# Turning the rows of x in the prologue: products with a diagonal of reciprocal roots in place of a scaling pass and transposes

## The chip, the cores and the metric

The kernel runs on one core of a Trainium2 chip. The metric is device microseconds (us) of one execution. Three runs of the kernel before gave 1731.33, 1733.20 and 1735.08 us, median 1733.2. In the rows, PE is TensorE's matmul, PEld its weight load, DVE is VectorE, ACT is ScalarE, POOL is GpSimd and SP is the queue of SyncE, from which nearly all loads are issued. L248 is line 248 of the kernel before.

## What is computed

One decoder block on x of 1024 rows by 1024 channels, all in float32. Only the beginning matters here:

```python
mod = silu(c) @ w_ada + b_ada                      # 6 x 1024 numbers
sh1, sc1, g1, sh2, sc2, g2 = split(mod, 6)
h = rms_norm(x, norm_mix_g) * (1.0 + sc1) + sh1    # x * rsqrt(mean(x*x) + eps) * g ...
proj = h @ w_in + b_in                             # 1024 x 1024 times 1024 x 8200
```

After that come a gated convolution of 31 taps, a chunkwise mLSTM, merge gates, an output projection and a gated FFN. They are not touched.

## The kernel before

Every big product runs as three float32r products: an operand is split into a rounded part and a rest (`hi` and `lo` of the weights, `hh` and `hl` of h), and hi by hh, hi by hl and lo by hh are summed in PSUM. For such a product the contraction must lie on partitions, so h is needed turned: channels on partitions, rows along the free dimension. Eight tiles `xT[k]` of 128 channels by 1024 rows hold the turned, normalised x; `hh[k]` and `hl[k]` are made from them.

The prologue (lines 183 to 367) makes all that. Its parts, in the order of the code:

- Loads on SP, in this order: x (`xt`, four pieces of two row tiles), small parameter rows, the first group of the modulation weights (`wad`, `load_ada(0)`, 2 MB in four loads), two raw weight tiles of the first two product blocks (`raws`, L139), then `load_ada(1)` to `load_ada(3)`.
- For each half q of the rows (four row tiles): ACT squares and sums each tile (L235), DVE and POOL make the reciprocal roots (L237, L104), each row tile is scaled in place (L242 on ACT for one tile, L244 on DVE for seven), then for each of eight channel tiles k four transposes on PE fill one PSUM bank (L248, `pn` for k = 0, 3, 6, two buffers of `pc` for the others), and a copy moves the bank to `xT[k]` (L251). Of the 16 copies ACT makes 13 and DVE 3 (`EVAC`).
- `split_rest` makes hi and lo of the two raw weight tiles (L148 on ACT, L149 on DVE).
- The modulation in four groups g of two channel tiles. `mod_sums(g)` is eight DVE steps over `wad[g]` (L275, L277) into `macc`; `mod_products(g)` sums it over partitions with four float32 products by a column of ones (L283, eight records on PE); `mod_cols(g)` is four small ACT steps that make the columns `sh1` and `G1` (L292, L293).
- For each group then `high(k)` on ACT (`hh`, L297), `full(k)` on ACT (L300, in place on `xT`) and a subtraction on DVE (`hl`, L336); for the last group DVE makes the full value itself (L340, L343). `first_products(g, 0)` is 16 products with `hh` and `first_products(g, 1)` eight with `hl` (L308), for the first two blocks at once, into two PSUM tiles `first[0]` and `first[1]`.

The order on each engine is written out by hand: three lists `on_v`, `on_s` and `on_t` hold groups of instructions for DVE, ACT and PE, and `in_turn` queues each group behind the one before it. On PE the order is `first_products(g, 0)`, `mod_products(g + 1)`, `first_products(g, 1)`. On DVE it is, for each g, `mod_sums(g + 1)` and then the two subtractions. What is in no list is placed by the planner of the language, by its own model of durations. Last, `param_columns` turns four tiles of later parameter rows through the single PSUM buffer `pa` (L125, L128).

After the prologue `glu_gate` reads `first[0]` on ACT (a sigmoid, L412), which frees the PSUM tile into which the third block of products (L158) runs. From there on PE works almost without a break to the end.

Of the kernel before, what the change touches and what calls it, by code (L numbers as in the profile page):

```python
# [17 lines left out]
KT = 8  # L18
# [17 lines left out]
SCALE = "vvvvvvva"  # L36
EVAC = ("aaaaaaaa", "avaavaav")
# [11 lines left out]
def hybrid_block(ctx: ExitStack, tc: tile.TileContext, x, c, w_ada, b_ada, norm_mix_g, w_in, b_in,  # L49
# [72 lines left out]
    def param_columns(rows):  # L122
        group, plan, t = rows
        p = ps_a()
        nc.tensor.transpose(p[:, 0:128], t, ident)  # L125
        n = sum(n for _, _, n in plan)
        col = const.tile([128, n], F32, name=f"col{group}")
        nc.vector.tensor_copy(col, p[:, 0:n])  # L128
        at = 0
        for key, ap, n in plan:  # L130
            cols[key] = col[:, at:at + n]
            at += n
# [52 lines left out]
    rows = pro.tile([128, 8, 128], F32, name="rows", tag="rows", bufs=2)  # L185
# [3 lines left out]
    xt = []  # L189
# [25 lines left out]
    def split_rest():  # L215
        for i in range(2):
            load_split(None, 0, KT, 0, *w_first[i], raw=raws[i])
# [11 lines left out]
    late_evac = {"v": [], "s": []}  # L229
    rstd = pro.tile([128, 3, 8], F32, name="rstd")  # L230
    xT = [big.tile([128, S], F32, name=f"xT{k}", tag="xb") if k < XB else pro.tile([128, S], F32, name=f"xT{k}") for k in range(KT)]
    for q in range(2):
        for t in range(4 * q, 4 * q + 4):
            junk = ps_mm()
            nc.scalar.activation(flat(junk), xt[t], AF.Square, accum_out=rstd[:, 0, t:t + 1])  # L235
        ms, rs, sc = (rstd[:, i, 4 * q:4 * q + 4] for i in range(3))
        nc.vector.tensor_scalar(ms, ms, 1.0 / D, EPS, op0=OP.mult, op1=OP.add)  # L237
        rsqrt(rs, ms)
        for t in range(4 * q, 4 * q + 4):
            r = rstd[:, 1, t:t + 1]  # L240
            if SCALE[t] == "a":
                nc.scalar.activation(xt[t], xt[t], AF.Copy, scale=r)  # L242
            else:
                (nc.gpsimd if SCALE[t] == "p" else nc.vector).tensor_scalar(xt[t], xt[t], r, None, op0=OP.mult)  # L244
        for k in range(KT):
            p = ps_n() if k % 3 == 0 else ps_c()
            for t in range(4):
                nc.tensor.transpose(p[:, t * 128:(t + 1) * 128], xt[q * 4 + t][:, k * 128:(k + 1) * 128], ident)  # L248
            h = xT[k][:, q * 512:(q + 1) * 512]
            e = "s" if EVAC[q][k] == "a" else "v"  # L250
            ins = nc.scalar.activation(h, p, AF.Copy) if e == "s" else nc.vector.tensor_copy(h, p)  # L251
            if q and k > 1:
                late_evac[e].append(ins)
# [48 lines left out]
    def first_products(g, kind):  # L302
        ks = (2 * g, 2 * g + 1)
        x = hl if kind else hh
        steps = [(i, k, n) for n in ((0,) if kind else (0, 1)) for k in ks for i in range(2)]
        if g == 3 and kind:
            steps.sort(key=lambda step: step[0])
        return [nc.tensor.matmul(flat(first[i])[:, a:b], w_first[i][n][:, k, :], x[k][:, a:b],  # L308
                                 start=(g == 0 and k == 0 and n == 0 and not kind), stop=(g == 3 and k == KT - 1 and kind == 1))
                for i, k, n in steps for a, b in HALVES]  # L310
# [5 lines left out]
    on_v.append(parts[1])  # L316
    on_v.append(late_evac["v"])
    on_s.append(late_evac["s"])
    split_rest()
    p, ins = mod_products(0, acc)  # L320
    for g in range(4):
# [8 lines left out]
        else:  # L330
            w_next[0] = wp.tile([128, KT, 128], F32R, name="whi", tag="whi"), wp.tile([128, KT, 128], F32R, name="wlo", tag="wlo")
            raw_next = load_raw(win, 0, KT, GLU_B + 128)
        if g < 3:
# [11 lines left out]
        if g == 2:  # L345
            rows = pro.tile([128, 8, 128], F32, name="rows", tag="rows", bufs=2)
# [11 lines left out]
        on_t.append(first_products(g, 0))  # L358
        if g < 3:
# [5 lines left out]
    for rows in later:  # L365
        param_columns(rows)
# [970 lines left out]
```

## Time and profile before

| | us |
|---|---|
| median of three runs | 1733.2 |
| profiled execution, its own time | 1735.88 |
| its span, first instruction to last | 1734.1 |
| PE busy in the span | 1692.9 (98%) |
| DVE busy | 1249.7 (72%) |
| ACT busy | 611.7 (35%) |
| start of the first L158 product | 61.59 |

The span of the profiled execution is 1.8 us shorter than its time, which is what lies around it. In a row of the timeline the columns are start and duration in us, engine, line, operation, what is written and read, how many were merged, and in brackets the idle time before with what ended it. The granted clock is a share of TensorE's full speed of 2.4 GHz. Ends of matmuls are modelled, so pace is read from starts.

### The profile page before, as it was taken

Reading aid. Unit: us, or ns where it says so; the run is one execution under the profiler, and the core shown is the slowest. Engines: PE = TensorE matmul, PEld = TensorE weight load, DVE = VectorE, ACT = ScalarE, POOL = GpSimd, SP = SyncE. Lnnn points to the kernel's source line nnn. Section 1 sums busy time; section 2 is a strip of 40 time slices with the busy share of each in tenths; the row PEclk is TensorE's granted clock in tenths of the full one; section 3 lists DMA queues with packets and bytes.
Section 4 is the critical chain, followed back from the end, with each engine's and each line's share of the span. In section 5 each row is a group of like instructions: output and inputs, shape, how many; then the busy total and the mean of one; then the engine's idle time right before and its main releaser. Section 6 shows DMA issues by size and latency. Waiting matters only on the chain. (4 is left out here: it accounts for less than half of the span.)

```text
span 1734.1 us, 20875 instructions
## 1 busy us (share of the span) xinstructions
PE 1692.9 (98%) x8360; PEld 1418.6 (82%) x8360; DVE 1249.7 (72%) x1681; ACT 611.7 (35%) x809; POOL 52.7 (3%) x113
## 2 busy tenths in 40 slices
PE   5999999999999999999999998999999999999998
PEld 4788889888988888888888778888888888778887
DVE  6989998997799669446798668766666665685243
ACT  7424335323433253223522386322222222232122
POOL 0000001000001000000000000000000000000000
PEclk9999999999999999999999999999999999999999
DMA  9221120221111112243694743322222222653121
GB/s 320 63 62 49 37 71 28 61 73 49 37 49 61 61 49 61 73 146 98 209 376 167 230 152 104 98 86 85 86 73 75 84 81 96 226 168 101 58 94 52
DMA packets 194711, 179.91 MB, mean 104 GB/s; under 512 B 7463, under 2 KB 166711, under 8 KB 194615
## 3 DMA queue, kind: packets, MB, share of 16 engines
q1 hardware_dynamic: 177367, 146.61, 27.4%
q10 hardware_dynamic: 17248, 31.99, 5.0%
q8 instruction: 65, 1.06, 0.3%
q14 instruction: 31, 0.25, 0.0%
HBM read 146.06 MB, written 32.51 MB: 103 GB/s over the span
## 5 line engine op out<-in xcount | busy, mean ns | idle before, releaser
L388 DVE SCALAR_TENSOR_TENSOR cacc<-a,col,cacc 128x1024 f32<-128x1024 f32 x240 | 306.8, 1286 | 3.9 <-ACT cacc L386 1.4
L158 PE MATMUL mm<-hh,wlo 128*128 128x512 f32 x864 | 271.2, 391 | 1.5 <-DVE wlo L149 1.5
L158 PE MATMUL mm<-hl,whi 128*128 128x512 f32 x864 | 272.5, 392 | 0.0
L158 PE MATMUL mm<-hh,whi 128*128 128x512 f32 x864 | 271.6, 392 | 0.0
L158 PEld LDWEIGHTS mm<-hh,wlo 128*128 128x128 f32 x864 | 160.3, 188 | 33.6 <-DVE wlo L149 2.7
L158 PEld LDWEIGHTS mm<-hl,whi 128*128 128x128 f32 x864 | 161.0, 188 | 32.1 <-issue 0.5
L158 PEld LDWEIGHTS mm<-hh,whi 128*128 128x128 f32 x864 | 160.5, 188 | 31.6
L148 ACT ACTIVATE whi<-wraw 128x1024 fp32r<-128x1024 f32 x61 | 64.7, 1061 | 226.5 <-PE mm L158 171.3
L149 DVE TENSOR_TENSOR wlo<-wraw,whi 128x1024 fp32r<-128x1024 f32 x61 | 74.5, 1222 | 28.7 <-ACT whi L148 25.2
L1114 PE MATMUL mm<-Bh,gh 128*128 128x512 f32 (+1 forms) x192 | 71.5, 375 | 2.9 <-ACT gh L1051 1.5
L1115 PE MATMUL mm<-Bl,gh 128*128 128x512 f32 (+1 forms) x192 | 71.5, 373 | 0.6 <-DVE Bl L1033 0.6
L604 PE MATMUL mm<-wlo,hh 128*128 128x256 f32 x256 | 72.0, 282 | 0.0
L1116 PE MATMUL mm<-Bh,gl 128*128 128x512 f32 (+1 forms) x192 | 71.2, 371 | 0.0
L1303 DVE TENSOR_TENSOR x<-x,mm 128x1024 f32<-128x1024 f32 x24 | 29.3, 1219 | 52.0 <-PE mm L1301 49.6
L1179 ACT ACTIVATE whi<-wraw 128x512 fp32r<-128x512 f32 (+2 forms) x32 | 25.3, 792 | 114.8 <-PE mm L1301 75.8
L535 DVE SCALAR_TENSOR_TENSOR cacc<-qkraw,col,cacc 128x1024 f32<-128x1024 f32 x48 | 61.5, 1282 | 4.9 <-ACT cacc L533 4.5
L603 PE MATMUL mm<-whi,hh 128*128 128x256 f32 x192 | 54.6, 284 | 0.0
L605 PE MATMUL mm<-whi,hl 128*128 128x256 f32 x192 | 54.2, 283 | 0.0
L1299 PE MATMUL mm<-fa,whi 128*128 128x512 f32 x128 | 50.6, 396 | 1.6 <-DVE cu L1142 0.9
L1300 PE MATMUL mm<-fa,wlo 128*128 128x512 f32 x128 | 50.5, 395 | 1.2 <-DVE wlo L1180 1.2
L1301 PE MATMUL mm<-fa,whi 128*128 128x512 f32 x128 | 50.6, 395 | 0.0
L1052 DVE TENSOR_TENSOR ul<-uraw,uh 128x1024 fp32r<-128x1024 f32 x20 | 24.5, 1225 | 35.4 <-ACT uh L1051 35.4
(444 smaller groups left out, 3893.1 us busy)
## 6 DMA issues: line engine op xcount, KB each, us to landing
wraw<-in_w_in_dram SPq DMA_DIRECT2D x64, 512.0 KB
awt<-in_w_ada_dram SPq DMA_DIRECT2D x32, 512.0 KB
graw<-in_w_ffn_up_dram SPq DMA_DIRECT2D x24, 512.0 KB
uraw<-in_w_ffn_up_dram SPq DMA_DIRECT2D x22, 512.0 KB
draw<-in_w_ffn_down_dram SPq DMA_DIRECT2D x22, 512.0 KB
act_d<-cg ACTq DMA_DIRECT2D x38, 256.0 KB
wad<-in_w_ada_dram SPq DMA_DIRECT2D x16, 512.0 KB
wraw<-in_w_out_dram SPq DMA_DIRECT2D x16, 512.0 KB
```

What stands on the lines that cost most here:

```text
L148: nc.scalar.activation(hi, raw, AF.Copy)
L149: (eng or nc.vector).tensor_sub(lo, raw, hi.bitcast(F32))
L158: nc.tensor.matmul(flat(acc)[:, a:b], lhs[:, k, :], rhs[k][:, a:b], start=(first and k == 0), stop=(last and k == kt - 1))
L388: nc.vector.scalar_tensor_tensor(acc, a[:, j:j + S], dw_col(j, ct), acc, op0=OP.mult, op1=OP.add)
L535: nc.vector.scalar_tensor_tensor(cv, raw[:, j:j + S], wcol(j), cv, op0=OP.mult, op1=OP.add)
L603: nc.tensor.matmul(o, hh[k][:, ts_], his[k], start=False, stop=False)
L604: nc.tensor.matmul(o[:, 0:256], hh[k][:, ts_], los[k], start=False, stop=False)
L605: nc.tensor.matmul(o, hl[k][:, ts_], his[k], start=False, stop=(k == KT - 1))
L1114: nc.tensor.matmul(o, a, rh, start=(k == 0), stop=False)
L1115: nc.tensor.matmul(o, a, rl, start=False, stop=False)
L1116: nc.tensor.matmul(o, b, rh, start=False, stop=(k == 3))
L1299: nc.tensor.matmul(o, hi[:, i, :], his[i][:, a:b], start=(i == 0), stop=False)
```

## The change

The scaling of the row tiles is gone. DVE instead makes, for each row tile, a 128x128 diagonal matrix of that tile's reciprocal roots (`diag`), and PE multiplies each block of x by it: a float32 product of a block with a diagonal is the block turned and scaled. All 16 copies out of PSUM are ACT's. In the written order DVE has all eight sums of group 0 first, then the lo parts of the first weights. PE has five of the second half's eight banks ahead of `mod_products(0)` and the other three between `first_products(0, 0)` and `mod_products(1)`. ACT has two of the second half's copies ahead of `mod_cols(0)`, three after `high(1)` and three ahead of `mod_cols(1)`. In the last group the products with `hh` and `hl` are reordered so that `first[0]` is complete eight products before the end. The tile `rows` has one buffer where it had two, and the last four turns of parameter rows go to four PSUM buffers. The diff, cut to its core:

```diff
-    rows = pro.tile([128, 8, 128], F32, name="rows", tag="rows", bufs=2)
+    rows = pro.tile([128, 8, 128], F32, name="rows", tag="rows")
...
     def split_rest():
+        out = []
         for i in range(2):
-            load_split(None, 0, KT, 0, *w_first[i], raw=raws[i])
+            hi, lo = w_first[i]
+            nc.scalar.activation(hi, raws[i], AF.Copy)
+            out.append(nc.vector.tensor_sub(lo, raws[i], hi.bitcast(F32)))
+        return out
...
+    diag = pro.tile([128, 8, 128], F32, name="diag")
...
         for t in range(4 * q, 4 * q + 4):
-            r = rstd[:, 1, t:t + 1]
-            if SCALE[t] == "a":
-                nc.scalar.activation(xt[t], xt[t], AF.Copy, scale=r)
-            else:
-                (nc.gpsimd if SCALE[t] == "p" else nc.vector).tensor_scalar(xt[t], xt[t], r, None, op0=OP.mult)
+            nc.vector.tensor_scalar(diag[:, t], ident, rstd[:, 1, t:t + 1], None, op0=OP.mult)
         for k in range(KT):
             p = ps_n() if k % 3 == 0 else ps_c()
-            for t in range(4):
-                nc.tensor.transpose(p[:, t * 128:(t + 1) * 128], xt[q * 4 + t][:, k * 128:(k + 1) * 128], ident)
-            h = xT[k][:, q * 512:(q + 1) * 512]
-            e = "s" if EVAC[q][k] == "a" else "v"
-            ins = nc.scalar.activation(h, p, AF.Copy) if e == "s" else nc.vector.tensor_copy(h, p)
-            if q and k > 1:
-                late_evac[e].append(ins)
+            turned = [nc.tensor.matmul(p[:, t * 128:(t + 1) * 128], xt[q * 4 + t][:, k * 128:(k + 1) * 128], diag[:, q * 4 + t],
+                                       start=True, stop=True) for t in range(4)]
+            copied = nc.scalar.activation(xT[k][:, q * 512:(q + 1) * 512], p, AF.Copy)
+            if q:
+                turns.append(turned)
+                copies.append([copied])
...
+        if g == 3:
+            if not kind:
+                return []
+            high = [(i, k, n, hh) for n in (0, 1) for k in ks for i in range(2) if n == 0 or i == 0]
+            steps = high + [s for s in steps if s[0] == 0] + [(1, k, 1, hh) for k in ks] + [s for s in steps if s[0] == 1]
...
-    on_v.append(parts[1])
-    on_v.append(late_evac["v"])
-    on_s.append(late_evac["s"])
-    split_rest()
+    on_v += parts
+    on_v.append(split_rest())
+    on_s += copies[:2]
+    on_t += turns[:5]
     p, ins = mod_products(0, acc)
+    on_t.append(ins)
...
+        if g == 0:
+            on_s += copies[2:5]
...
         on_t.append(first_products(g, 0))
+        if g == 0:
+            on_t += turns[5:]
+            on_s += copies[5:]
...
-    for rows in later:
-        param_columns(rows)
+    for rows, bank in zip(later, (ps_a, ps_n, ps_c, ps_c)):
+        param_columns(rows, bank)
```

## Rows read from the trace of the kernel before

**Rows 1.** The page: the span.
```profile
span 1734.1 us, 20875 instructions
```

**Rows 2.** Windows: start:end, length, busy us of each engine (x instructions), clock, DMA, GB/s.
```profile
16.50:26.90 10.40, 7.08 (x52) 5.46 (x52) 9.65 (x14) 9.46 (x16) 1.02 (x1) 1.00 1.13 328
26.90:30.90 4.00, 1.12 (x10) 0.99 (x9) 3.89 (x8) 2.10 (x6) 0.00 (x0) 0.90 1.09 348
30.90:37.00 6.10, 6.10 (x14) 4.76 (x15) 5.85 (x7) 3.33 (x3) 0.00 (x0) 0.50 1.09 349
37.00:61.60 24.60, 23.79 (x112) 18.00 (x110) 22.87 (x30) 18.30 (x26) 0.22 (x2) 1.00 0.42 115
61.60:1734.00 1672.40, 1651.30 (x8163) 1386.82 (x8162) 1202.71 (x1607) 567.05 (x740) 49.74 (x103) 1.00 0.31 98
```

**Rows 3.** Timeline of PE: sums over partitions, products of the first blocks, third block.
```profile
27.71 1.05 PE L283 MATMUL pa<-ones_col,macc 128*128 128x1 f32 x8 [0.77 <-DVE macc L277]
30.88 6.74 PE L308 MATMUL mm<-hh,wf 128*128 128x512 f32 x16 [2.12 <-ACT hh L297]
37.46 0.95 PE L283 MATMUL pa<-ones_col,macc 128*128 128x1 f32 x8
...
51.58 1.04 PE L283 MATMUL pa<-ones_col,macc 128*128 128x1 f32 x8
...
58.86 1.99 PE L308 MATMUL mm<-hl,wf 128*128 128x512 f32 x8
...
61.59 0.73 PE L158 MATMUL mm<-hh,whi 128*128 128x512 f32 x2
```

**Rows 4.** Timeline of DVE: the last seven sums of group 3.
```profile
46.04 5.47 DVE L277 SCALAR_TENSOR_TENSOR macc<-wad,sc_c,macc 128x512 f32<-128x512 f32 x7
```

**Rows 5.** Lines of DVE, 0 to 62 us: count, busy us, mean ns, idle before.
```profile
L277 DVE SCALAR_TENSOR_TENSOR macc<-wad,sc_c,macc 128x512 f32<-128x512 f32 x28 | 21.0, 751 | 0.9
L336 DVE TENSOR_TENSOR hl<-xT,hh 128x1024 fp32r<-128x1024 f32 x6 | 7.3, 1221 | 0.3
L244 DVE TENSOR_SCALAR xt<-xt,rstd 128x1024 f32<-128x1024 f32 x7 | 4.8, 748 | 1.6 <-POOL rstd L104 1.6
...
L251 DVE COPY xT<-pc 128x512 f32<-128x512 f32 x3 | 2.0, 688 | 0.0
...
L237 DVE TENSOR_SCALAR rstd<-rstd 128x4 f32<-128x4 f32 x2 | 0.3, 170 | 1.9 <-ACT mm L235 1.9
```

**Rows 6.** Timeline of PE: transposes early and later.
```profile
12.85 0.48 PE L248 MATMUL pn<-ident,xt 128*128 128x128 f32 x1 [3.84 <-DVE xt L244]
13.11 0.63 PE L248 MATMUL pc<-ident,xt 128*128 128x128 f32 x2
...
19.88 1.14 PE L248 MATMUL pc<-ident,xt 128*128 128x128 f32 x8
```

**Rows 7.** Timeline of PE near 792 us: float32 products of 512 columns.
```profile
792.40 1.02 PE L832 MATMUL pn<-t4b,ones_d 128*128 128x512 f32 x2
793.26 1.02 PE L832 MATMUL pc<-t4b,ones_d 128*128 128x512 f32 x2
```

**Rows 8.** Timeline of ACT: a weight split, columns and high parts, the sigmoid.
```profile
23.35 1.06 ACT L148 ACTIVATE wf<-wraw 128x1024 fp32r<-128x1024 f32 x1 [0.23 <-DMA wraw<-in_w_in_dram]
...
28.80 0.26 ACT L292 ACTIVATE sh<-pa,mod_b 128x1 f32<-128x1 f32 x1 [2.07 <-PE pa L283]
...
29.58 2.38 ACT L297 ACTIVATE hh<-xT,sh,G 128x1024 fp32r<-128x1024 f32 x2
...
55.70 1.06 ACT L341 ACTIVATE whi<-wraw 128x1024 fp32r<-128x1024 f32 x1
...
60.42 1.11 ACT L412 ACTIVATE t<-mm,col 128x1024 f32<-128x1024 f32 x1 [1.41 <-PE mm L308]
```

**Rows 9.** Lines of ACT, 0 to 62 us: copies out of PSUM.
```profile
L251 ACT ACTIVATE xT<-pc 128x512 f32<-128x512 f32 x7 | 3.9, 593 | 0.3 <-PE pc L248 0.3
```

**Rows 10.** Timeline of SP: the issue of the next raw weights.
```profile
45.34 1.01 SPq L139 DMA_DIRECT2D wraw<-in_w_in_dram  x2
```

More of the change, by code (lines that the diff above doesn't have):

```diff
@@ L35 @@
 AT = (43, 43, 46, 49, 20, 20, 49, 49, 17, 24, 66, 64)
-SCALE = "vvvvvvva"
-EVAC = ("aaaaaaaa", "avaavaav")
 KX = 6
@@ L120, in param_rows, with param_columns @@
         return group, plan, t
-    def param_columns(rows):
+    def param_columns(rows, bank=ps_a):
         group, plan, t = rows
-        p = ps_a()
+        p = bank()
         nc.tensor.transpose(p[:, 0:128], t, ident)
@@ L227, in dw_col @@
         return cols["dw0"][:, r:r + 1] if r < 128 else cols["dw1"][:, r - 128:r - 127]
-    late_evac = {"v": [], "s": []}
+    turns, copies = [], []
     rstd = pro.tile([128, 3, 8], F32, name="rstd")
+    diag = pro.tile([128, 8, 128], F32, name="diag")
     xT = [big.tile([128, S], F32, name=f"xT{k}", tag="xb") if k < XB else pro.tile([128, S], F32, name=f"xT{k}") for k in range(KT)]
@@ L235, in hybrid_block @@
             nc.scalar.activation(flat(junk), xt[t], AF.Square, accum_out=rstd[:, 0, t:t + 1])
-        ms, rs, sc = (rstd[:, i, 4 * q:4 * q + 4] for i in range(3))
+        ms, rs = (rstd[:, i, 4 * q:4 * q + 4] for i in range(2))
         nc.vector.tensor_scalar(ms, ms, 1.0 / D, EPS, op0=OP.mult, op1=OP.add)
@@ L304, in first_products @@
         x = hl if kind else hh
-        steps = [(i, k, n) for n in ((0,) if kind else (0, 1)) for k in ks for i in range(2)]
-        if g == 3 and kind:
-            steps.sort(key=lambda step: step[0])
+        steps = [(i, k, n, x) for n in ((0,) if kind else (0, 1)) for k in ks for i in range(2)]
+        if g == 3:
[3 more added lines that the diff above has]
+            steps = high + [s for s in steps if s[0] == 0] + [(1, k, 1, hh) for k in ks] + [s for s in steps if s[0] == 1]
         return [nc.tensor.matmul(flat(first[i])[:, a:b], w_first[i][n][:, k, :], x[k][:, a:b],
-                                 start=(g == 0 and k == 0 and n == 0 and not kind), stop=(g == 3 and k == KT - 1 and kind == 1))
-                for i, k, n in steps for a, b in HALVES]
+                                 start=(g == 0 and k == 0 and n == 0 and x is hh),
+                                 stop=(g == 3 and k == KT - 1 and x is hl))
+                for i, k, n, x in steps for a, b in HALVES]
     on_v, on_s, on_t = [], [], []
@@ L345, in hybrid_block @@
         if g == 2:
-            rows = pro.tile([128, 8, 128], F32, name="rows", tag="rows", bufs=2)
+            rows = pro.tile([128, 8, 128], F32, name="rows", tag="rows")
             later = [
```

## The prediction, made before the change was run

> **What bounds the kernel now.** I read the span first [rows 1], then the windows [rows 2]: after 61.6 us PE is busy 1651.3 of 1672.4 us, so nearly all that is left there is PE's own work, and what the prologue costs is the time at which the third block starts, 61.59 [rows 3]. A change in the prologue is worth what it moves that start. In 37.0 to 61.6 DVE is busy 22.9 of 24.6 us and PE 23.8 [rows 2]: two engines are nearly full, and the order of waits must say which is late.
>
> The timeline of PE gives the frame [rows 3]: sums over partitions (`mod_products`, below mp0 to mp3) start at 27.71, 37.46 and 51.58; mp1 to mp3 are 14.1 us for two groups, 7.06 each. The first waits for DVE's `macc`. The last starts 0.07 after DVE ends the last sum of group 3, 46.04 + 5.47 = 51.51 [rows 4]. So at both ends DVE is the late one. One group costs DVE eight sums (about 0.5 + 5.47 = 6.0) and two subtractions of 1.22, 8.4 us together [rows 4, 5], more than the 7.06 that PE and ACT take in turn; DVE is behind them at mp3 because it began late, at about 51.5 - 6.0 - 2 x 8.4 = 28.7. From mp3 to the third block it is 10.0 us: the last product of the prologue ends at 58.86 + 1.99 = 60.85, but the third block waits until the sigmoid (60.42 + 1.11 = 61.53) frees a PSUM tile [rows 3, 6].
>
> **What goes.** Seven scalings on DVE, 4.8 us, three copies, 2.0 us [rows 5], and one scaling on ACT. A diagonal of 128x128 on DVE costs between 0.17 (the 128x4 form) and 0.75 (the 128x1024 form it replaces) [rows 5]; in proportion to its columns I take 0.2, eight are 1.6. DVE loses about 5.2 us. ACT gains three copies of 0.59 [rows 7], 0.5 from start to start: 1.5 less the scaling. The first turn waits for one diagonal instead of one scaling and starts near 12.3 instead of 12.85 [rows 8].
>
> **What a turn costs on PE.** Two float32 products of 512 columns start 0.86 us apart, two records each [rows 9]; a quarter of the columns is 0.215 per product. Eight transposes take 1.14, about 0.12 each in their banks [rows 8]. A bank of four turns thus goes from 0.5 to 0.9 us with a little for the change of bank. This is at full clock. The first transposes come slower, two in 0.63 [rows 8], and the stretch from 30.9 to 37.0 is granted 0.50 (1.2 GHz) after PE was busy 1.12 us in the 4.0 before; from 16.5 it is granted 1.00 (2.4 GHz) [rows 2]. At the lower level a bank costs 1.7.
>
> A rule that speaks against the change: the Trainium skill (TensorE: Matmul & The Clock Gate, Terms) calls the transpose mode four times faster for FP32. By it a product would cost 4 x 0.12 = 0.5, a bank 1.9 and 13 banks 25 us, an estimate; the rows here give less than twice. What that would do is the mechanism of the slower rival below.
>
> **The sum, step by step.**
> - mp0 now stands behind thirteen banks. From 12.3 at the lower level to 16.5 are 2.4 banks; the other 10.6 at 0.9 take until 26.0. Bounds: 24.0 at full level throughout, 34.5 at the lower. The sums of group 0, first on DVE now, end near 24 and don't bind. I take 26.0 to 26.5, against 27.71.
> - From mp0 to the first product it was 30.88 - 27.71 = 3.2 us (records, four column steps, one `high`) [rows 3, 6]; nothing of that changes: 29.3.
> - The pause between mp0's end and that product stays 2.1 us [rows 3], now after dense work. Before, the sixteen products after it took 6.58 instead of 16 x 0.23 = 3.6 [rows 3]. I take half of the slow stretch, 5.3, so 34.6. Then come the three late banks, 2.7, and mp1 is at 37.2 against 37.46. Bounds: 35.5 at full level, 39.4 with the whole slow stretch of 6.1 us.
> - DVE meanwhile. The second raw weight tile lands at 23.35 [rows 6]; `wad(1)`, 2.1 MB at 348 GB/s [rows 2], 6.0 us later at 29.4, its first half at 26.4. The last four sums of group 1 then end at 29.4 + 3.2 = 32.6. The subtractions need `full(0)` on ACT: columns at 27.3, two `high` of 1.14, three copies of 0.5, `full(0)` of 1.14 give 33. Sums of group 2 run from 35.3 to 41.3, some 1.8 earlier than before (51.5 - 6.0 - 2.4 - 6.0 = 37.1). But `full(2)` comes mp1 + 5.2 = 42.4 (records 1.0, columns 0.8, three passes of 1.14): DVE waits 1.1, which gives most of it back. Sums of group 3 end at 42.4 + 2.4 + 6.0 = 50.8; PE by its own turn comes to mp3 at 37.2 + 14.1 = 51.3 or a little less. I take 51.0, 0.6 earlier.
> - The tail. `first[0]` is complete eight products, 1.8 us, before the end, which covers 1.11 of sigmoid and the latency seen. The wait of 61.59 - 60.85 = 0.7 goes; PE's own products are late next.
> Sum: 0.6 + 0.7 = 1.3 us. At full level throughout DVE doesn't wait for `full(2)`: mp3 at 49.6, 2.0 + 0.7 = 2.7. With the whole slow stretch mp3 is at 53.4 and the sum 1.1 us later than before.
>
> Costed at nothing, with their cover: the four late turns of parameter rows and their copies (PE's pauses; 0.3 us each if they come in line); the two memsets of the second `rows` tile, which now waits until the first is read near 15 us (0.17 each on DVE); the loads behind them on SP, among them the next raw weights, issued at 45.34 [rows 10] and read at 55.70 [rows 6], with some 5 us of room after they land. On ACT a weight split queued ahead of copies would hold them until the tile lands; the PSUM banks give it about one bank, 0.9.
>
> The sum is made on the profiled execution, 1735.88 us, which would be 1734.6; that execution lies 2.7 above the median of the three runs, so I carry the difference over: 1733.2 - 1.3 = 1731.9.
>
> **Rivals.** This kernel's measurement can tell about 0.2%, 3.5 us, from no change.
> - Full clock: the pause of 2.1 us doesn't lower the grant. For it: PE is denser before the pause than it was. Against: 26.9 to 30.9 [rows 2], where 1.12 us of work in 4.0 was followed by 0.50. 1733.2 - 2.7 = 1730.5.
> - Slower: turns decide. If PE runs the products at the lower level to the end, or a product costs four transposes, mp0 is at 34.5 and everything after it 8 us later; the sum is 6 to 9 us against it, 1740.7. The point from which it decides: gain is gone when mp0 is 1.3 later than taken, at 27.5, so when thirteen banks take over 15.2 us, 1.17 each. For it: the early pairs of transposes at 0.63. Against: transposes already raised the grant by 16.5, and products are denser.
> - Nothing: ACT, with more copies and the same splits, or the late parameter turns on PE, hand back 1.3 us. 1733.2.
> - More: DVE, 5.2 us lighter, goes into the long part with a lead. There PE has 21 us without work [rows 2]; if a quarter goes, 1731.9 - 5 = 1726.9. Against: PE follows its own order there, and that idle time is in small pieces behind many engines.
>
> **How the numbers follow.** Forecast 52%, full clock 20%, slower 7%, nothing 13%, more 8%. The predicted time is the forecast's, 1731.9. Its own bounds reach from 1730.5 to 1734.3; the three runs of before differ by up to 1.9 from their median, so the range is 1728.0 to 1735.5, which leaves out most of the slower and the larger case and some of the edges. Faster by over 3.5 us: all of the largest case, about half of the full clock's, a tenth of the forecast's, 0.23. Slower by over 3.5: the slower case and 2% from the edges, 0.09. Within: 0.68.
>
> **What would show it.** Right: turns of 0.2 us per product from about 17 us on, mp0 between 25.5 and 27, `full(0)` and then DVE's subtractions near 33, a DVE wait for `full(2)` of about 1 us, mp3 near 51, no wait of PE between `first[1]` and the third block, and that block at 60.3. Wrong: mp0 after 27.5 (the turns), sums of group 1 late (the loads), mp3 before 49.5 (something else bound it), or a start near 60.3 with a median that has moved by more than 3 us: then the long part has changed.

## The result, and the profile after

The changed kernel is slower, by 0.2 to 0.3%. Against runs of the kernel before its median was 1739.03 us to 1732.78 (eight runs each). The comparison puts the ratio at 1.0028 with a 95% interval of 1.0019 to 1.0037; the bare ratio of the two medians, 1.0036, lies near the upper end of it. Two later comparisons gave 1.0028 (1.0018 to 1.0038) and 1.0021 (1.0012 to 1.0030). The forecast was 1731.9 with a range of 1728.0 to 1735.5, so the time moved the other way and lies outside the range. In the rows section four groups stand under other numbers than the prediction gives them: its [rows 6] is the group printed as Rows 8, its 7 is Rows 9, its 8 is Rows 6 and its 9 is Rows 7; this section and the next ones use the printed numbers.

The profiled execution of the changed kernel took 1735.75 us. It is the fastest of its eight and as long as the profiled one of before (1735.88), so the two profiles compared whole show no loss; what they do show is where the time goes in the prologue. Lines of its page and its windows, in the columns of [rows 2] (line numbers are always those of the kernel that ran: L246 here is L248 of the kernel before):

```profile
span 1734.0 us, 21003 instructions
PE 1697.1 (98%) x8424; PEld 1425.0 (82%) x8424; DVE 1244.6 (72%) x1679; ACT 611.4 (35%) x811; POOL 52.5 (3%) x113
...
16.50:26.90 10.40, 10.40 (x87) 10.27 (x86) 8.61 (x21) 7.43 (x12) 1.02 (x1) 1.00 1.13 328
26.90:30.90 4.00, 1.88 (x15) 1.66 (x13) 3.42 (x6) 2.88 (x6) 0.00 (x0) 1.00 1.09 350
30.90:37.00 6.10, 6.10 (x26) 4.84 (x25) 5.86 (x8) 4.22 (x7) 0.00 (x0) 0.72 1.09 349
37.00:61.60 24.60, 23.04 (x116) 17.54 (x115) 22.00 (x29) 18.72 (x28) 0.00 (x0) 1.00 0.36 104
61.60:1734.00 1672.40, 1651.03 (x8170) 1386.28 (x8168) 1202.66 (x1607) 566.83 (x741) 49.82 (x105) 1.00 0.31 99
```

DVE has become lighter, as it should: 1244.6 us busy in the span where it had 1249.7, 5.1 for the 5.2 put down. PE now works through all of 16.5 to 26.9, and in 37.0 to 61.6 it is a little less busy than before (23.04 us for 23.79). What counts is PE's timeline, which answers to [rows 3] and [rows 6]:

```profile
12.31 0.80 PE L246 MATMUL pn<-diag,xt 128*128 128x128 f32 x2 [3.20 <-DVE diag L243]
...
16.74 1.06 PE L246 MATMUL pc<-diag,xt 128*128 128x128 f32 x4
...
18.74 1.95 PE L246 MATMUL pc<-diag,xt 128*128 128x128 f32 x16
20.53 1.06 PE L246 MATMUL pn<-diag,xt 128*128 128x128 f32 x8
...
27.03 0.95 PE L281 MATMUL pa<-ones_col,macc 128*128 128x1 f32 x8
30.09 5.74 PE L309 MATMUL mm<-hh,wf 128*128 128x512 f32 x16 [2.12 <-ACT hh L295]
...
38.34 0.95 PE L281 MATMUL pa<-ones_col,macc 128*128 128x1 f32 x8
...
43.33 0.31 PE L123 MATMUL pn<-ident,rows 128*128 128x128 f32 x1 [0.72 <-DMA rows<-in_conv_dw_w_dram]
...
46.26 0.27 PE L123 MATMUL pc<-ident,rows 128*128 128x128 f32 x1
47.03 0.30 PE L123 MATMUL pc<-ident,rows 128*128 128x128 f32 x1 [0.51 <-DMA rows<-in_qk_conv_w_dram]
47.17 0.95 PE L281 MATMUL pa<-ones_col,macc 128*128 128x1 f32 x8
...
54.24 0.95 PE L281 MATMUL pa<-ones_col,macc 128*128 128x1 f32 x8
...
61.30 1.98 PE L309 MATMUL mm<-hl,wf 128*128 128x512 f32 x8
64.03 0.73 PE L156 MATMUL mm<-hh,whi 128*128 128x512 f32 x2 [0.75 <-ACT t L420]
```

The third block starts at 64.03 instead of 61.59: 2.44 us later, where 1.3 earlier was forecast. Read the four sums over partitions (L281): mp0 is 0.68 earlier than before and mp1 0.88 later. Between mp1 and mp2 lie 8.83 us, where before every group took 7.06, and from mp2 to mp3 it is 7.07 again. So it is the stretch from 38.3 to 47.2 that is too long, and three instructions stand in it that were not there before: L123, turns of the late parameter rows. Two of them wait for their loads, 0.72 and 0.51 us. DVE's timeline shows copies of such turns, which wait for PE in their turn, and the sums of group 3 behind the second:

```profile
43.68 0.29 DVE L126 COPY col<-pn 128x128 f32<-128x128 f32 x1 [1.36 <-PE pn L123]
...
47.38 0.29 DVE L126 COPY col<-pc 128x128 f32<-128x128 f32 x1 [0.35 <-PE pc L123]
47.58 5.47 DVE L275 SCALAR_TENSOR_TENSOR macc<-wad,sc_c,macc 128x512 f32<-128x512 f32 x7
```

The queue of SP shows when these loads are issued, the first and the last of twelve, and under them the last one in the kernel before:

```profile
37.10 0.36 SPq L116 DMA_DIRECT2D rows<-in_conv_dw_w_dram  x1
...
44.55 0.55 SPq L116 DMA_DIRECT2D rows<-in_qk_conv_w_dram  x1
```

```profile
44.06 0.55 SPq L118 DMA_DIRECT2D rows<-in_qk_conv_w_dram  x1
```

The load that the turn at 43.33 waits for was issued at 37.1 or 38.5, while the `wad` loads still filled the DMA engines (share 1.09 in the row up to 37.0). The turn that reads the last load can't come before about 47, 2.5 us after its issue; mp2 was wanted at 45.4 (38.34 + 7.06). The Trainium skill (DMA: Bandwidth & Descriptors, section Anatomy of one DMA — SWDGE (gpsimd) path) gives a transfer a fixed cost of about 2.0 us, measured there for GpSimd's issue; these rows, on SP's, show 2.5 from the start of the issue (44.55) and 1.9 from its end (45.10) to the product that waits for it (47.03), which agrees with it roughly.

Last the tail. The sigmoid that answers to the one of [rows 8] still waits for PE:

```profile
62.86 1.11 ACT L420 ACTIVATE t<-mm,col 128x1024 f32<-128x1024 f32 x1 [1.28 <-PE mm L309]
```

It starts 0.42 before PE's last product ends (61.30 + 1.98 = 63.28), just as before (60.42 against 60.85), and the third block waits 0.75 for it.

### The profile page after: what moved, and what is told of

Its sections match the earlier page's. It is cut to its first block, busy times and chain, and to the rows that moved or that the text cites. A ratio compares the mean times of both kernels' runs of the same rounds, so it can differ in the third digit from the quotient of the medians.

```text
span 1734.0 us, 21003 instructions
## 1 busy us (share of the span) xinstructions
PE 1697.1 (98%) x8424; PEld 1425.0 (82%) x8424; DVE 1244.6 (72%) x1679; ACT 611.4 (35%) x811; POOL 52.5 (3%) x113
## 4 chain that ended last, share of the span: by engine, by line
PE 87%; DVE 5%; DMA 4%; issue 2%; SPq 2%; ACT 1%; POOL 0%; POOLq 0%; ACTq 0%; DVEq 0%
PE mm L156 39%; PE mm L1122 5%; PE mm L1123 4%; PE mm L1124 4%; PE mm L1308 2%; PE mm L1309 2%; PE mm L1307 2%; PE mm L611 1%; PE mm L613 1%; PE mm L612 1%; PE pc L1122 1%; PE pc L1124 1%; PE pc L1123 1%; SPq L199 1%; PE pa L1123 1%
## 5 line engine op out<-in xcount | busy, mean ns | idle before, releaser
L543 DVE SCALAR_TENSOR_TENSOR cacc<-qkraw,col,cacc 128x1024 f32<-128x1024 f32 x48 | 61.5, 1282 | 5.0 <-ACT cacc L541 4.5
```

## The experiments

All comparisons are with runs of the kernel before on the same chip; a1 and e1 to e3 ran on one chip, the other runs of the table on a second. The ratio is that of the comparison and can differ a little from that of the two medians. "Third block" is the start of the first product behind the prologue and "rest" is the span less that, both from the one profiled execution. Before has 61.59 and 1672.6. The diffs are cut to what matters, with `...` for what is left out.

| label | what it is | median us (runs) | before | ratio, 95% interval | third block | rest |
|---|---|---|---|---|---|---|
| a1_after_again | changed kernel | 1738.78 (9) | 1734.08 | 1.0028 (1.0018 to 1.0038) | 63.88 | 1673.9 |
| e1_one_bank | changed, late turns through one buffer | 1738.77 (10) | 1734.08 | 1.0023 (1.0014 to 1.0032) | 61.62 | 1674.3 |
| e2_late | changed, late turns queued late | 1735.37 (11) | 1734.08 | 1.0011 (1.0003 to 1.0020) | 62.36 | 1671.3 |
| e3_before_banks | before, four buffers for the late turns | 1736.30 (11) | 1734.08 | 1.0010 (1.0001 to 1.0019) | 65.95 | 1670.1 |
| e4_products_only | before, turns by products | 1737.19 (11) | 1734.32 | 1.0016 (1.0007 to 1.0025) | 64.14 | 1671.3 |
| e6_pause | changed, three repairs | 1736.05 (11) | 1734.32 | 1.0009 (1.0000 to 1.0018) | 61.22 | 1674.5 |
| e8_old_order | e1 with the order of before behind the prologue | 1734.86 (11) | 1734.32 | 1.0008 (0.9998 to 1.0017) | 62.14 | 1673.3 |
| e9_new_order | before with e1's order behind the prologue | 1735.46 (11) | 1734.32 | 1.0009 (1.0000 to 1.0018) | 61.61 | 1671.6 |
| e10_after_old_order | changed with the order of before behind the prologue | 1738.15 (11) | 1734.13 | 1.0020 (1.0011 to 1.0029) | 64.02 | 1672.0 |
| e11_before_new_order | before with the changed kernel's order behind the prologue | 1734.45 (11) | 1734.13 | 1.0001 (0.9992 to 1.0010) | 61.48 | 1670.2 |
| a2_after_third | changed kernel | 1738.10 (11) | 1734.13 | 1.0021 (1.0012 to 1.0030) | 63.73 | 1669.4 |
| a0_before_again | before | 1734.95 (11) | 1734.13 | 1.0004 (0.9995 to 1.0012) | 61.53 | 1672.6 |

### The late turns of parameter rows

The theory after the first profile: the four PSUM buffers let the planner place the late turns ahead of mp2, where they wait for loads. Its rivals were that the products with the diagonals themselves cost the time, and that it is lost behind the prologue. The changed kernel ran again beside three edits:

> The changed kernel once more, unchanged. Its first profile has the third block at 64.03 us, 2.44 later than before, and a granted clock of 0.998; most of its other executions were granted 0.994 to 0.996 and took 3 us more. Theory 'prologue': the loss of about 6 us in the median is the 2.4 us of the prologue and the grant, which falls more often than before; a second profile then shows the third block within 0.5 us of 64.0 and further stretches at 0.50, and the spans go with the grant, some 1.7 us per stretch of 3.4 us. Theory 'long part': the loss lies after the third block at equal grant; then the stretch from the third block to the end is over 1671 us even where the grant is 1.00 in it (1670.0 in the first profile).

e1_one_bank takes the late turns back to the one buffer `pa`, which the sums over partitions use as well:

```diff
-    for rows, bank in zip(later, (ps_a, ps_n, ps_c, ps_c)):
-        param_columns(rows, bank)
+    for rows in later:
+        param_columns(rows)
```

> The changed kernel, with the four late turns of parameter rows through the one buffer pa again, as before; all else of the change stays. Theory 'late rows': with free PSUM buffers the planner queues three of these turns on PE ahead of mp2 (and their copies on DVE among the subtractions and the sums), where they wait for their loads; PE lost about 1.8 us there (8.83 us from mp1 to mp2 instead of 7.06). Then mp2 comes 7.1 after mp1, the third block at 61.5 to 62.2, and the median 1.5 to 3 us below the changed kernel's. Theory 'products': the dear turns on PE lose the time; then the third block stays within 0.5 us of 64.0.

e2_late keeps the four buffers and writes down where the turns stand, on PE behind the products of group 2 and on DVE behind the subtractions:

```diff
         on_t.append(first_products(g, 1))
+        if g == 2:
+            late_cols = [param_columns(rows, bank) for rows, bank in zip(later, (ps_a, ps_n, ps_c, ps_c))]
+            on_t.append([turn for turn, _ in late_cols])
...
+            on_v.append([late_cols[0][1]])
...
+            on_v.append([copy for _, copy in late_cols[1:]])
...
-    for rows, bank in zip(later, (ps_a, ps_n, ps_c, ps_c)):
-        param_columns(rows, bank)
```

> The changed kernel with four buffers, but the four late turns queued by hand on PE behind the products of group 2 with hl, and their copies on DVE behind the last subtractions. Theory 'late rows': as with one buffer, mp2 7.1 after mp1 and the third block at 61.5 to 62.3. Theory 'products': no change within 0.5 us. If the number of buffers matters by itself (a bank not free in time), this one is late and the one with a single buffer is not.

e3_before_banks gives the kernel before the four buffers, and nothing else of the change:

```diff
-    def param_columns(rows):
+    def param_columns(rows, bank=ps_a):
...
-        p = ps_a()
+        p = bank()
...
-    for rows in later:
-        param_columns(rows)
+    for rows, bank in zip(later, (ps_a, ps_n, ps_c, ps_c)):
+        param_columns(rows, bank)
```

> The kernel before, with only the four buffers for the late turns of parameter rows. Theory 'late rows': the planner does the same here, some turns stand ahead of mp2 or mp3 and wait for their loads; the third block comes 1 to 3 us after 61.59 and the median rises by as much. If the four buffers only help, as the prediction held, PE's 0.4 us wait for pa is gone and the third block comes at 61.2 to 61.6.

PE's timeline, first of e1, then of e2, then of e3:

```profile
37.67 0.95 PE L281 MATMUL pa<-ones_col,macc 128*128 128x1 f32 x8
...
44.73 0.95 PE L281 MATMUL pa<-ones_col,macc 128*128 128x1 f32 x8
...
61.62 0.73 PE L156 MATMUL mm<-hh,whi 128*128 128x512 f32 x2
```

```profile
38.20 0.95 PE L282 MATMUL pa<-ones_col,macc 128*128 128x1 f32 x8
...
45.26 0.95 PE L282 MATMUL pa<-ones_col,macc 128*128 128x1 f32 x8
...
62.36 0.73 PE L157 MATMUL mm<-hh,whi 128*128 128x512 f32 x2 [0.75 <-ACT t L424]
```

```profile
43.29 0.30 PE L125 MATMUL pn<-ident,rows 128*128 128x128 f32 x1 [2.22 <-DMA rows<-in_conv_dw_w_dram]
...
46.71 0.95 PE L283 MATMUL pa<-ones_col,macc 128*128 128x1 f32 x8
...
54.77 1.05 PE L283 MATMUL pa<-ones_col,macc 128*128 128x1 f32 x8 [0.81 <-DVE macc L277]
...
65.95 0.73 PE L158 MATMUL mm<-hh,whi 128*128 128x512 f32 x2 [0.75 <-ACT t L412]
```

In e1 and e2 mp2 comes 7.06 after mp1, and the third block is back at 61.6 and 62.4. In e3 the first late turn stands at 43.29 as in the changed kernel, PE waits 2.22 for its load, and the third block goes from 61.59 to 65.95. So it is the place of the late turns, which the four buffers let the planner choose: with the buffers alone the kernel before has its third block 4.4 later (e3), and with the buffers but the turns put elsewhere the changed kernel gets most of it back (e2). This step is shown. The time of e2 fell with it, by 3.4 us against a1. Two medians do not follow the third block. That of e1 did not fall, although its third block starts where that of before does; that was the next question. That of e3 rose by 2.2 us only, where its third block came 4.4 later; its one profile has a stretch granted 0.50 (1.2 GHz) from 56.0 on, 3.4 us long, which its other executions need not have; why its median rose less stays open.

### The products alone

e4_products_only is the kernel before with products by the diagonal in place of scaling and transposes (and the one `rows` buffer); copies, orders and late turns stay:

```diff
-            r = rstd[:, 1, t:t + 1]
...
+            nc.vector.tensor_scalar(diag[:, t], ident, rstd[:, 1, t:t + 1], None, op0=OP.mult)
...
-                nc.tensor.transpose(p[:, t * 128:(t + 1) * 128], xt[q * 4 + t][:, k * 128:(k + 1) * 128], ident)
+                nc.tensor.matmul(p[:, t * 128:(t + 1) * 128], xt[q * 4 + t][:, k * 128:(k + 1) * 128], diag[:, q * 4 + t],
+                                 start=True, stop=True)
```

> The kernel before with one part of the change: products with the diagonals in place of scaling and transposes; banks, copies, orders and late turns as before (the rows tile has one buffer). The prediction's term: DVE saves its seven scaling passes less eight small ones ahead of the first sums, PE pays no more for a bank at the full clock. Theory 'products pay': mp0 at 26.5 to 27.0 and the third block at 60.3 to 61.0. Theory 'nothing': third block at 61.6 within 0.3. If the products' lower share of work raises the clock later than the transposes did: 62.5. The time behind it: the planner's order in the long part differs in 689 PE instructions, so by 'planner' the time may be off by 2 to 4 us either way whatever the third block does; by 'clock' it follows the third block, 1733 to 1734.

mp0 stayed at 27.70 and the third block came at 64.14. DVE's timeline tells why:

```profile
30.59 0.69 DVE L249 COPY xT<-pc 128x512 f32<-128x512 f32 x1 [2.09 <-PE pc L245]
31.19 0.48 DVE L273 TENSOR_SCALAR macc<-wad,sc_c 128x512 f32<-128x512 f32 x1
```

A bank of products takes 0.9 us on PE where a bank of transposes takes 0.5, so the last banks come later, and DVE, which still makes three copies in that order, waits 2.09 for one of them with all sums of group 1 behind it (31.19, before 28.77). 'Products pay' falls: without the other parts of the change, the copies on ScalarE and the new order, the products bring the third block 2.5 us later.

### The tail and the pause

e6_pause has e2's repair and two more. The last group's products are queued in fours, so that the planner keeps their order, and the three late turns of x move into PE's pause ahead of the first products:

```diff
-    on_s += copies[:2]
+    on_s += copies[:5]
...
     on_t.append(ins)
+    on_t += turns[5:]
...
-        if g == 0:
-            on_s += copies[2:5]
...
-            on_t += turns[5:]
...
-        on_t.append(first_products(g, 1))
+        last = first_products(g, 1)
+        on_t += [last] if g < 3 else [last[j:j + 4] for j in range(0, len(last), 4)]
```

> The changed kernel with three repairs of the prologue: the late turns of parameter rows queued on PE behind the products of group 2 and their copies on DVE behind the subtractions; the last group's products held in the written order; the three late turns of x moved into PE's pause ahead of the first products, and five copies ahead of the columns of group 0. Behind the prologue the planner's order is nearly that of before (26 PE and 3 DVE instructions differ). Sum from the traces: first products at 31 as in e2 (bound by the columns and high parts), mp1 some 1.5 to 2 earlier than e2's 38.20, no wait of 0.75 at the end: third block 59.5 to 60.5, against 61.6 of before. Theory 'planner': long part as before, so 1732.3 to 1733 (0.9988 to 0.9994). Theory 'clock': 1736 to 1737 in spite of the earlier third block.

PE's timeline, and two of its windows:

```profile
30.70 3.93 PE L310 MATMUL mm<-hh,wf 128*128 128x512 f32 x16
34.47 0.95 PE L282 MATMUL pa<-ones_col,macc 128*128 128x1 f32 x8
...
42.21 1.05 PE L282 MATMUL pa<-ones_col,macc 128*128 128x1 f32 x8 [0.51 <-DVE macc L276]
...
50.58 1.05 PE L282 MATMUL pa<-ones_col,macc 128*128 128x1 f32 x8 [1.06 <-DVE macc L276]
...
60.31 1.07 PE L310 MATMUL mm<-hl,wf 128*128 128x512 f32 x4
61.22 0.62 PE L157 MATMUL mm<-hh,whi 128*128 128x512 f32 x2
```

```profile
30.70:37.00 6.30, 6.30 (x34) 5.17 (x33) 6.05 (x8) 5.92 (x11) 0.00 (x0) 1.00 1.09 349
52.31:55.72 3.41, 3.41 (x12) 2.46 (x10) 2.48 (x5) 3.41 (x6) 0.00 (x0) 0.50 0.00 0
```

Three things can be read. With the order held, the third block follows the last product without a wait, so the 0.75 of the tail is a matter of order within the group. Without the pause the sixteen first products take 3.93 us at a granted clock of 1.00 (2.4 GHz), where behind a pause of 2.12 they took 5.74, and mp1 comes 3.7 us earlier than in e2. And the gain is then given back: DVE's sums set the pace again, PE waits 0.51 and 1.06 for them, and after the second wait a stretch is granted 0.50 (1.2 GHz). The third block is only 0.4 earlier than before, where 59.5 to 60.5 had been expected, and the median is not below that of before.

### Is it the planner's order behind the prologue?

e1 was as slow as the changed kernel with a third block at 61.6. The code behind the prologue is the same, but the planner orders it by its own clock, so a changed prologue can change that order: 237 of 8121 PE instructions stand elsewhere in e1, 213 in the changed kernel, all near 275 to 306 and near 1045 to 1070 us. These four kernels take one kernel's prologue and fix the other's order behind it, by queueing each instruction there behind the one that should stand before it (ORDER is a table of instruction numbers):

```diff
+    made = {int(i.name.split("-")[1]) - here: i for i in nc.cur_bb.bb.instructions}
+    for runs in ORDER:
+        turn = [made[n] for a, b in runs for n in range(a, b)]
+        for a, b in zip(turn, turn[1:]):
+            tc.add_manual_dep(b, a.name, mybir.DependencyInfo(mybir.DependencyClass.NoSync, mybir.DependencyReason.DATA),
+                              reason="order")
```

> The changed kernel with the late turns through one buffer (as e1_one_bank, whose third block starts at 61.6 like that of before, and which is still 4.7 us slower in the median), and with the order of PE, DVE and ACT behind the prologue fixed to that of before: the planner had put 237 of 8121 PE, 41 of 1600 DVE and 23 of 769 ACT instructions elsewhere, all of them near 275 to 310 and near 1045 to 1070 us. Theory 'planner': that order costs the 3 to 5 us; the time is then that of before, 1734 (ratio 1.000, within 0.001), third block 61.6, rest 1670.5. Theory 'clock': the order costs nothing, the prologue leaves another pattern of dips of the granted clock; the time stays at 1738.8 (1.0025), with a mean clock of .995 where before has .9965.

> The other way round: the kernel before, with its own prologue, and the order behind it fixed to that of e1_one_bank (those same instructions). Theory 'planner': 3 to 5 us slower than before, 1738 (1.0020 to 1.0028), third block 61.6, rest 1674. Theory 'clock': as before, 1734 (within 0.0007).

For e1 the theory held in part. With the order of before its ratio went from 1.0023 to 1.0008, measured on two chips and with intervals that just overlap, and e1's order cost the kernel before 1.1 us, barely clear of nothing. The place is seen in PE's timeline near 305, first before, then e9, with e9's window behind it:

```profile
305.04 0.73 PE L158 MATMUL mm<-hh,wlo 128*128 128x512 f32 x2 [0.79 <-DVE wlo L149]
```

```profile
304.93 1.05 PE L167 MATMUL mm<-hh,wlo 128*128 128x512 f32 x2 [1.87 <-DVE wlo L158]
305.16:308.57 3.41, 3.41 (x9) 2.62 (x9) 3.41 (x5) 0.00 (x0) 0.00 (x0) 0.50 0.59 154
```

DVE's split of a weight tile comes late there, the pause grows from 0.79 to 1.87, and the grant falls to 0.50 right behind it; e1 has the same pause (1.86) and the same stretch. That is most of what e1 loses in its profile: its rest is 3.0 us longer than the mean of four executions of before, of which at most 0.5 are there ahead of that pause and 2.8 behind the stretch. But the changed kernel has another order than e1, and it had to be asked for by itself, in a square of both prologues and both orders:

> The changed kernel with the order behind the prologue fixed to that of before (213 of 8121 PE, 37 of 1600 DVE and 21 of 769 ACT instructions stand elsewhere in the changed kernel, near 275 to 306 and near 1045 to 1070 us). With e11_before_new_order and the two kernels themselves it is a square: either prologue with either order. Theory 'planner': of the 4.7 to 6.2 us that the change costs, 2.4 are the third block's later start and the rest is that order: 1736.4 to 1737 here (ratio 1.0012 to 1.0016). Theory 'prologue': the order is worth nothing and all of it follows from the prologue, by the third block and by the clock's dips: 1739 (1.0028) as the changed kernel.

> The other corner of the square: the kernel before, with the order behind its prologue fixed to that of the changed kernel. Theory 'planner': 2 to 3.5 us over before, 1736.3 to 1738 (1.0012 to 1.0020), with a pause of 1.3 us on PE near 305 where before has 0.8. Theory 'prologue': as before, within 0.0007. The sum of this and of e10_after_old_order's difference should be the changed kernel's own if the two causes only add.

> The changed kernel itself, for the square on one chip: 1738.8 to 1739 (1.0028), third block at 63.9 to 64.0. Of its pauses near 305, 998, 1043, 1495 and 1553 us those that come from its order should stand as in the two profiles at hand (1.3 near 305, 0.5 near 1495); those that come from the landing of a load should scatter (near 998 and 1043).

> The kernel before, unchanged, for a second profile of it: the same time as its other runs (1.000 within 0.0007), third block at 61.6. If the pauses near 998 (1.04 in the first profile), 1043 (1.49) and the clock's dips near 272 and 1545 are matters of a single execution, they differ here; if they belong to the kernel, they stand.

Here 'planner' falls. With the changed prologue the time is 1738.15 under the order of before and 1738.10 under its own; with the old prologue it is 1734.45 and 1734.13. The order is worth nothing that these runs can tell (their intervals reach 1.5 us either way), and the whole 4 us go with the prologue.

### Where the rest of it goes

The third block's start accounts for 2.4 us of those 4. Six more executions, on a third chip, were profiled to find the remainder:

> The changed kernel once more, for a profile of an execution with a lower mean clock. Theory 'dips in the prologue': in such executions the first stretch of half clock lasts 6.8 us instead of 3.4 or a second one follows the waits at 43 and 47 us, and because PE sets the pace there the third block starts at 65.5 or later. Theory 'dips behind it': the third block starts at 63.7 to 64.0 as in the four profiles at hand, and stretches of half clock follow the pauses near 275, 305, 998 or 1043 us, each worth up to 1.7 us.

> The same question and the same expectations as a4_after_look: one more execution of the changed kernel, to see how the stretches of half clock and the waits for loads differ from execution to execution.

> The same question and the same expectations as a4_after_look: one more execution of the changed kernel.

> The same question and the same expectations as a4_after_look: one more execution of the changed kernel.

> The kernel before, one more profile. Seven profiles of the changed kernel have a part behind the third block's start (the rest) of 1669.4 to 1673.9 us, mean 1671.9; the two of before have 1672.6 both, in executions that were 1.7 us over its median. Theory 'longer rest': in ordinary executions of before the rest is 1670 to 1671. Theory 'same rest': it scatters about 1672 as the changed kernel's does, and the change has cost the prologue's 2.4 us alone.

> The same question and the same expectations as a8_before_look, with one more execution of the kernel before; also whether the first stretch of half clock is 3.4 or 6.8 us long and whether the third block's start of 61.5 to 61.6 depends on that.

All profiled executions of the two kernels; a stretch at half clock lasted 3.41 us unless a length is given, and the one at the very end is left out:

| kernel | own time | third block | rest | stretches granted 0.50, start |
|---|---|---|---|---|
| before | 1735.88 | 61.59 | 1672.6 | 30.1 (6.83), 272, 1546 |
| before, a0 | 1735.90 | 61.53 | 1672.6 | 31.4, 274, 1045 |
| before, a8 | 1732.63 | 61.52 | 1669.4 | 31.7 |
| before, a9 | 1734.08 | 61.56 | 1670.8 | 29.7 (6.83), 272 |
| changed | 1735.75 | 64.03 | 1670.0 | 31.5 |
| changed, a1 | 1739.52 | 63.88 | 1673.9 | 29.9, 276 |
| changed, a2 | 1734.86 | 63.73 | 1669.4 | 31.0 |
| changed, a4 | 1737.19 | 63.94 | 1671.5 | 31.2, 1001, 1045 |
| changed, a5 | 1739.22 | 64.02 | 1673.5 | 28.9, 275, 1002 |
| changed, a6 | 1738.98 | 64.05 | 1673.2 | 29.8, 276, 1003, 1047 |
| changed, a7 | 1737.63 | 63.87 | 1672.0 | 31.7, 1045 |

The third block's start hardly scatters: 61.55 in the mean against 63.93, a difference of 2.4. The rest scatters by 3.2 us in before and 4.5 in the changed kernel, with means of 1671.3 and 1671.9. 'Dips in the prologue' falls, since the first stretch is 3.41 long in all seven executions of the changed kernel; 'dips behind it' describes what is seen. Counted from the third block, PE reaches each line of the code within 0.3 us of before in the mean as far as 970 us (0.1 at 970), and 0.6 later from about 1091 on. The pause near 305 is longer in the changed kernel (1.24 to 1.26 us for 0.79 to 0.88), but it goes with the order (0.78 in e10) and leaves no loss by 970. The other place that differs lies where the 0.6 arises. PE waits near 974 and near 999 for splits of raw `w_out` tiles: 1.2 to 1.8 and then 0.6 to 1.1 in the four executions of before, but 0.5 to 0.7 and then 0.9 to 1.9 in the seven of the changed kernel. In three of these seven the clock falls behind the second pause, in none of before. Of a6, PE's timeline and the window:

```profile
1001.39 0.50 PE L1013 MATMUL mm<-wlo,y 128*128 128x512 f32 x1 [1.86 <-DVE wlo L1006]
1002.57:1005.98 3.41, 3.41 (x10) 2.65 (x9) 1.46 (x5) 2.89 (x5) 2.55 (x4) 0.50 0.84 274
```

What moves the wait from 974 to 999 was not found; the changed kernel keeps it under the order of before (0.80 and 1.61 in e10).

The profiled executions differ by 3.0 us in the mean of their own times, 2.4 in the prologue and 0.6 behind it; all executions together, 32 of the changed kernel and 118 of before on several chips, by 1738.55 - 1734.24 = 4.3. With seven and four profiles, each scattered by some 1.6 us, 3.0 and 4.3 can't be told apart. So up to about 1.3 us more than the profiles show may lie behind the prologue, and that stays open. The stretches at half clock within the prologue don't fill it. Two of the four executions of before have a first stretch of 6.83 instead of 3.41, and their third block starts no later (61.59 and 61.56 against 61.53 and 61.52): where the stretch is short, PE comes to mp3 early and waits about 1.0 there for DVE's sums. In the changed kernel all seven have the short one.

## Why the prediction was wrong

**What bounds the kernel** was read rightly in the main: of the 3.0 us between the profiles of the two kernels 2.4 are the third block's start. As a rule it does not hold: e1's third block starts with that of before, and its median is 4.7 us longer, a good part of it by the planner's order behind the prologue. Right too was that the start of the prologue would be PE's. The rest follows the sum.

- **Turns and mp0.** Right in kind. A bank went from 1.7 to 0.9 us as put down (in the timeline four records from 16.74 to 17.59, sixteen from 18.74 to 20.53), a diagonal took 0.21 of DVE (1.7 us for eight), and a copy 0.60 on ACT. Forecast for mp0 was 26.0 to 26.5; the seven executions have 26.2 to 27.1, in step with the moment at which the pace doubles: 15.2 in the one with the earliest mp0 (a5), 18.1 in the one with the latest (a7) and 17.8 in the profile above, where 16.5 had been taken. The rule of the Trainium skill (TensorE: Matmul & The Clock Gate, Terms) that the transpose mode is four times faster for FP32 is not borne out here: eight transposes of [rows 6] take 1.14 us, eight records of products, which are only four turns, 1.06: about 1.9 times per turn, and not four times.
- **From mp0 to mp1.** Right in kind, short in size. The pause was 2.1, half the slow stretch followed (3.41 us for 6.83), and the sixteen products took 5.6 (forecast 5.3, though half of what 6.58 had over 3.6 makes 5.1); mp1 came at 38.3 in the profiled execution and at 37.1 to 38.5 in all seven, forecast 37.2. Most of the difference is mp0's. 'Full clock' did not come: it held that the pause does not lower the grant, and in all seven executions the grant falls late in the pause or up to 1.5 us behind it. What it would have been worth e6 shows, where the pause is filled: 3.93 for these products.
- **mp2: the step that failed.** The prediction costed the late turns "at nothing", covered by PE's pauses, "0.3 us each if they come in line". They came in line, and they brought the wait for their loads with them. mp2 is then set by those loads and not by anything before it. Two executions, a5 and a7, show that with mp1 at 37.11 and at 38.47:

```profile
43.35 0.30 PE L123 MATMUL pn<-ident,rows 128*128 128x128 f32 x1 [1.97 <-DMA rows<-in_conv_dw_w_dram]
...
47.16 0.95 PE L281 MATMUL pa<-ones_col,macc 128*128 128x1 f32 x8
```

```profile
43.22 0.30 PE L123 MATMUL pn<-ident,rows 128*128 128x128 f32 x1 [0.48 <-DMA rows<-in_conv_dw_w_dram]
...
47.02 0.95 PE L281 MATMUL pa<-ones_col,macc 128*128 128x1 f32 x8
```

  mp2 is at 47.0 to 47.2 in both, and at 46.9 to 47.2 in all seven. By the forecast it would have been at 37.2 + 7.06 = 44.3: however early mp1 had come, the loads held mp2 back until 2.8 us after that. The rows for it lay in the trace of before: SP issued the last of these loads at 44.06, and the one buffer `pa` that held the turns back was in the code. I looked at what the turns cost, and not at what the single buffer kept them from.
- **DVE.** Sums of group 1 waited for `wad` as forecast (0.47) and ended at 33.9, not 32.6. The wait of 1.1 for `full(2)` came as forecast: in the changed kernel it lies under the 1.36 that a copy ahead of it waits for its turn, and e2, where the late turns stand elsewhere, shows it on DVE's timeline:

```profile
43.50 2.55 DVE L342 TENSOR_TENSOR hl<-xT,hh 128x1024 fp32r<-128x1024 f32 x2 [1.20 <-ACT xT L299]
```

  It costs the third block nothing there, since in e2 PE comes to mp3 (52.32) behind DVE's last sum (46.49 + 5.47 = 51.96).
- **The tail: the second step that failed.** The 0.7 didn't go. The written order holds groups of instructions behind one another, and inside a group of 24 products the planner chose its own; e6 shows that the gain is real once the order is held.
- **Sum.** Forecast 60.3, measured 64.0. Of the 3.7 us, 1.1 were there at mp1 (38.34 for 37.2), 2.1 came from mp1 to mp3 (15.9 for 13.8) and 0.5 behind it (9.8 for 9.3). The late turns are not all that kept the gain away: with them put right, e2's third block starts at 62.36, still 0.8 behind that of before, since mp1 is 0.7 later there than before's (38.20 for 37.46) and the wait of the tail stands.
- **Rivals.** The slower one named the wrong mechanism: its point was mp0 later than 27.5, and mp0 was earlier. The 34.5 that it gives for mp0 is that of the lower level; its other branch, by the prediction's own estimate of 25 us for thirteen banks, would have been at 37. 'Nothing' came nearest: it spoke of the late turns on PE, but held them good for 1.3 us at most. 'More' was wrong in sign; DVE's lead brought the long part nothing (rest 1671.9 against 1671.3).
- **The range** took in the bounds of the steps that had a price (one is off: the whole slow stretch gives mp1 29.3 + 6.6 + 2.7 = 38.6 and not 39.4). A step put at nothing has no bound, and both that failed, the late turns and the wait of the tail, were of that kind.

No version here beats the kernel before. e2, e6 and e8 take back most of the loss; e6 has the earliest third block (61.22) and still not a lower median.

## What to carry to other kernels

A buffer that several users share is an order as well: before giving one of them buffers of its own, look up when its inputs land and which queue the planner may now move it ahead of. An order that matters inside a group must be written inside the group. And what a delay on PE costs depends on what sets the pace behind it: in the kernel before mp1 lies between 36.2 and 37.5 and the third block at 61.5 to 61.6 all the same, because DVE's sums come last, while in e2 the 0.5 by which mp1 is later than in e1 is still there at mp3 (52.32 for 51.83).

## What was not expected of the hardware

- A grant of 0.50 came behind pauses of PE of only 1.06 (e6, at 50.6) to 2.1 us. The same pause of 1.8 near 275 was followed by one in some executions and not in others of the same kernel (in a5, not in a2).
- From 12.3 to 17.8 us the records of the products start 0.21 us apart and from then on 0.11, though a window gives a granted clock of 1.00 for either part. The trace's first record of the granted clock lies at 17.9 (at 15.3 in a5, where the pace doubles at 15.2), so the 1.00 ahead of it is no reading. The pace of a kernel's start is read from the starts.
- A pause of PE did not always lower the grant at once: the 2.1 us ahead of the first products did in all seven executions of the changed kernel, but e4 pauses 1.71 ahead of its first products, and the sixteen of them still take 4.14 us; its stretch at half clock comes at 48.3.
